# Adding the old state of a chunked recurrence in PSUM, scaling it once for each direction, and running the end of one pair of heads beside the first chain of the next

## The chip, the cores and the metric

The kernel runs on one core of a Trainium2 chip. TensorE is PE in the rows (PEld is its weight load), VectorE is DVE, ScalarE is ACT, GpSimd is POOL, and SyncE is SP, which issues the DMAs from one queue. The metric is the device time of one execution in microseconds; less is better. Before the change three runs gave 2336.16, 2346.11 and 2348.5 us, median 2346.11.

## The reference

Two residual blocks of two layers each on 512 tokens of width 1024; the second block also has 256 context tokens. The change lies in the even mixer of the second block: a linear recurrence over 768 tokens (256 of context, 512 latent) with twelve heads of 64, run forward and backward.

```python
def rwkv7_scan(r, w, k, v, kk, bb, s0, reverse):
    def step(s, inp):
        r_t, w_t, k_t, v_t, kk_t, b_t = inp
        sa = jnp.einsum('bhij,bhj->bhi', s, kk_t)
        s = s * w_t[:, :, None, :] - sa[..., None] * b_t[:, :, None, :] + v_t[..., None] * k_t[:, :, None, :]
        return s, jnp.einsum('bhij,bhj->bhi', s, r_t)
    ...
    for d in range(2):
        ...
        s_ctx, yc = rwkv7_scan(*tc[:6], zeros, d == 1)
        _, yl = rwkv7_scan(*tl[:6], s_ctx, d == 1)
def finish(o, gate_r, four, gate_f):
    mean = jnp.mean(o, axis=-1, keepdims=True)
    var = jnp.mean(jnp.square(o - mean), axis=-1, keepdims=True)
    o = ((o - mean) * lax.rsqrt(var + RWKV_GN_EPS)).reshape(b, l, RWKV_W) * lnx_g + lnx_b
    yr = o * jax.nn.silu(gate_r)
```

## The kernel before, in words

`rwkv` works on six pairs of heads (m = 0 to 5). The 128 partitions hold the two heads of a pair, 64 channels each. The 768 tokens are 12 chunks of 64, handled in three groups of four (g = 0, 1, 2), so there are 18 units of work q = 3m + g. Each unit goes through these stages, each a Python generator:

- `prep` (`inner_first`): decays and scaled keys, on ACT and DVE.
- `system` (`products`, `keys_by_token`): the products within a chunk; their triangular part goes through HBM (`lt`), POOL inverts its 16 by 16 blocks (`sN`, `sX`, `sT`), and the inverse comes back through HBM (`td`) to the tiles `T` and `DB`.
- `inverse` (`inner_rest`, `inner_second`): the 64 by 64 inverse out of these blocks, on PE (L1758), and `WT`.
- `chain`: the recurrence itself, four steps s, each with one chunk of the forward direction (d = 0) and one of the backward (d = 1). A step multiplies the old state `S` with `WT` into the PSUM tile `u` (L1822), copies `u` times -0.5 to `VU` (ACT for d = 0, DVE at L1829 for d = 1), multiplies `bkT` with `VU` into the PSUM tile `sp` (L1843), and makes the new state. Before, ACT writes the scaled old state `gs` for each direction, and four DVE instructions of 64x64 (L1851) form `sp * gc + gs`, one for each head and direction. `S` is block diagonal in the two heads. After the last step the outputs are gathered in the PSUM tile `misc` and go to `y`.

Each pair also has `pair_start` (token-major values, normalised keys) and `pair_end` (the bonus term, a normalisation over 64 channels, transposes at L1929, the gate, a store to `o_save`). `weave` emits the generators in turn. Between their steps it takes a step of `Feed`, 0.35 of one for each step of a generator: the projection matmuls of later pairs (`acc` tiles, L363 to L365, three for each slice of the depth), whose weight panels `ws` come through the SP queue. `Feed` takes its tasks strictly in the order of the list `order` and stops at one that `allow` has not yet set free; `feed.need` emits tasks until the named one is done. The framework then orders each engine's instructions by readiness. Each engine runs its own in that order.

PSUM has eight banks here: two for `acc0`, one for `acc1`, one for `misc`, two for `c`, one for `u` and one for `sp`. `misc` is shared by `prep`, `chain`, `pair_start` and `pair_end`.

Of the kernel before, what the change touches and what calls it, by code (L numbers as in the profile page):

```python
# [18 lines left out]
P = 128  # L19
# [254 lines left out]
class Program:  # L274
# [1013 lines left out]
    def rwkv(self, hl, hc):  # L1288
# [3 lines left out]
        with tc.tile_pool(name="rk", bufs=1) as rp:  # L1292
# [80 lines left out]
            order = [(0, n) for n in ("k0", "v", "r")]  # L1373
            for m in range(NH2):
                if m + 1 < NH2:
                    order.append((m, "gate"))
                    order += [(m + 1, n) for n in ("k0", "v", "r")]
            tasks = [task(*o) for o in order]
            tasks += [fourier_task(0, "four"), fourier_task(1, "four"), task(NH2 - 1, "gate"), fourier_task(0, "gate"), fourier_task(1, "gate")]
            feed = Feed(self, tasks, KT, xs)  # L1380
# [20 lines left out]
            for q in range(nq):  # L1401

                m, g = divmod(q, 3)
                gens = [self.chain(g, inner[q], pairs[m]), inverse(q + 1)]
                if g == 0:
                    if m:
                        feed.need((m - 1, "gate"))
                    run(self.pair_end(m - 1, pairs[m - 1]) if m else iter(()), system(q + 2), rate=RATE)
                    if m:
                        allow(m, "gate")  # L1410
                    start = ()
                    if m + 1 < NH2:
                        feed.need((m + 1, "v"))
                        start = self.pair_start(m + 1, pairs[m + 1])
                        feed.need((m + 1, "r"))
                    gens.append(chain(start, prep(q + 3)))
                else:
                    gens += [system(q + 2), prep(q + 3)]
                if q == nq - 1:

                    w = [rp.tile([P, 2, 2, 256], F32, tag="VU", name="dftx", bufs=2), self.E[1].rearrange("p a b -> p (a b)")]
                    for t, n in zip(w, ("k_dftx", "k_dftc")):
                        nc.sync.dma_start(out=t, in_=self.C[n])
                    feed.need(("gate", 0))
                    a = [rp.tile(sh, F32, tag=t, name=t, bufs=2) for t, sh in (("vT", [P, 6, P]), ("ks", [P, TT]))]
                    a[1] = a[1].rearrange("p (j n) -> p j n", n=P)
                    dft = lambda i, tag: self.dft(i, four["four", i], four["gate", i], a, tag, *w, tables)
                    gens.append(dft(0, "c"))
                run(*gens, rate=RATE)
                inner[q] = None  # L1430
                if g == 0:
                    allow(m + 2, "v")
                    if q == nq - 6:
                        feed.allowed.update((("four", 0), ("four", 1)))
                if g == 2:
                    allow(m + 2, "r")
                    allow(m + 3, "k0")
                    if q == nq - 4:
                        feed.allowed.update((("gate", 0), ("gate", 1)))
                if q == nq - 2:  # L1440
                    tables = [rp.tile([P, 4, T], F32, tag="m", name="m", bufs=3) for _ in range(2)]
                    for i in range(2):
                        nc.sync.dma_start(out=tables[i], in_=self.C["k_dftl"][:, :, i, :])
# [354 lines left out]
    def chain(self, g, st, pr):  # L1798
# [5 lines left out]
        Dm, VU, gc, M = self.DB, st["VU"], st["gc"], st["M"]  # L1804
        if g == 0:
            self.state = None
            pr["y"] = rp.tile([P, 6, P], F32, tag="y", name="y")
        y = pr["y"]
        u = self.psum("u", (P, 2, 2, P))
        for d, h, j, e in self.units():  # L1810
            R = half(1 - e)
# [3 lines left out]
        for s in range(4):  # L1815
# [16 lines left out]
            nxt = self.S[self.turn % len(self.S)]  # L1832
            self.turn += 1

            if S is not None:
                gs = rp.tile([P, 2, P], F32, tag="gs", name="gs")
                for d in range(2):
                    self.act(gs[:, d, :], S[:, d, :], AF.Copy, scale=gc[:, d, cs[d]:cs[d] + 1])
            yield
            sp = self.psum("sp", (P, 2, 64))  # L1840
            for d in range(2):
                for h in range(2):
                    nc.tensor.matmul(sp[half(h), d, :], st["bkT"][d][:, cs[d], half(h)], VU[:, d, cs[d], half(h)], start=True, stop=True)  # L1843
            for h in range(2):
                H = half(h)
                for d in range(2):
                    gd = gc[H, d, cs[d]:cs[d] + 1]
                    if S is None:
                        nc.vector.tensor_scalar(out=nxt[H, d, H], in0=sp[H, d], scalar1=gd, scalar2=None, op0=ALU.mult)
                    else:  # L1850
                        nc.vector.scalar_tensor_tensor(out=nxt[H, d, H], in0=sp[H, d], scalar=gd, in1=gs[H, d, H], op0=ALU.mult, op1=ALU.add)  # L1851
            self.state = nxt
            yield
        yield
        ps = self.psum("misc", (P, 4, P))

        last = None
# [33 lines left out]
    def pair_end(self, m, pr):  # L1891
# [29 lines left out]
        yield  # L1921
        tt(out=y4, in0=y4, in1=bc(s1), op=ALU.subtract)
        yield
        tt(out=y4, in0=y4, in1=bc(s2), op=ALU.mult)
        yield
        for a, b in ((0, 4), (4, 6)):
            ps = self.psum("misc", (P, 4, P))
            for j in range(a, b):
                nc.tensor.transpose(ps[:, j - a, :], y[:, j, :], self.k_ident)  # L1929
            self.act(ks[:, a * P:b * P], ps[:, :b - a, :].rearrange("p a b -> p (a b)"), AF.Identity, scale=col(cols["lgh"]), bias=col(cols["lbh"]))  # L1930
            yield
        tt(out=gate, in0=gate, in1=ks, op=ALU.mult)
# [288 lines left out]
```

## Time and profile before

| | us |
|---|---|
| median of three runs | 2346.11 |
| the profiled execution | 2352.9 |
| its span, first to last instruction | 2351.1 |
| the recurrence, about 1200 to 1912 us in the span | 712 |
| PE busy in the span | 2187.3 |
| mean granted clock of PE | 0.959 |

The granted clock is a share of 2.4 GHz: 1.00 in a stretch is 2.4 GHz throughout, 0.50 is 1.2 GHz. In rows of a timeline the first number is the start in us, the second the time to the end of the last of the xN merged instructions. An entry in brackets is how long the engine sat idle before and who released it. Matmuls are pipelined, so starts that follow each other give the pace, and the duration of one is longer.

### The profile page before, as it was taken

The numbers are of one execution on the slowest core, as the hardware profiler recorded it, in microseconds if no ns is written. First come the engines' busy times: TensorE is split into PE (matmuls) and PEld (weight loads), VectorE is DVE, ScalarE is ACT, GpSimd is POOL, SyncE is SP. The second block draws the span as 40 slices with busy tenths as digits, with TensorE's granted clock in tenths as the row PEclk, the third lists the DMA queues.
The fourth block names the chain that finished last, engine by engine and source line by source line (L and its number), as shares of the span: only waits on it lengthen the run. The fifth ranks groups of instructions, "written<-read, shape, count | busy, mean of one in ns | idle before, by whom it ended". The sixth has DMA issues, their size and how long they took to land. (4 is left out here: it accounts for less than half of the span.)

```text
span 2351.1 us, 40197 instructions
## 1 busy us (share of the span) xinstructions
PE 2187.3 (93%) x15774; PEld 1752.6 (75%) x15774; DVE 1623.3 (69%) x3014; ACT 1077.8 (46%) x2033; POOL 337.3 (14%) x722
## 2 busy tenths in 40 slices
PE   6889989999998999999898999999899999999996
PEld 4667768878775788888676677777677777888885
DVE  6799886568859787444675868787866556555544
ACT  3466353223335332333564545556554355655542
POOL 1321020000002000000004232332413100000001
PEclk9999999999999999999998979999998999999998
DMA  8433356566624656323322222212212242422211
GB/s 290 138 127 127 134 158 194 179 208 194 195 74 125 210 183 208 100 87 101 134 77 64 53 58 47 68 40 67 54 46 57 85 158 100 131 72 72 72 55 45
DMA packets 203742, 269.66 MB, mean 115 GB/s; under 512 B 125216, under 2 KB 137376, under 8 KB 203168
## 3 DMA queue, kind: packets, MB, share of 16 engines
q1 hardware_dynamic: 203552, 267.09, 37.3%
q8 instruction: 124, 2.03, 0.3%
q14 instruction: 66, 0.54, 0.1%
HBM read 250.38 MB, written 16.66 MB: 114 GB/s over the span
## 5 line engine op out<-in xcount | busy, mean ns | idle before, releaser
L363 PE MATMUL acc<-hh,wh 128*128 128x512 f32 x1416 | 574.9, 407 | 36.3 <-ACT wh L322 21.0
L365 PE MATMUL acc<-hh,wl 128*128 128x512 f32 x1416 | 571.9, 404 | 7.9 <-POOL wl L340 4.2
L364 PE MATMUL acc<-hl,wh 128*128 128x512 f32 x1416 | 572.7, 404 | 1.3 <-DVE hl L340 1.2
L322 ACT ACTIVATE wh<-ws 128x1024 fp32r<-128x1024 f32 (+4 forms) x307 | 275.8, 902 | 423.8 <-PE acc L364 313.4
L340 DVE TENSOR_TENSOR wl<-ws,wh 128x1024 fp32r<-128x1024 f32 (+3 forms) x294 | 305.3, 1041 | 202.6 <-ACT wh L322 193.7
L363 PEld LDWEIGHTS acc<-hh,wh 128*128 128x128 f32 x1416 | 271.4, 192 | 98.3 <-ACT wh L322 23.0
L365 PEld LDWEIGHTS acc<-hh,wl 128*128 128x128 f32 x1416 | 270.7, 191 | 74.6 <-DVE wl L340 8.4
L364 PEld LDWEIGHTS acc<-hl,wh 128*128 128x128 f32 x1416 | 271.6, 192 | 60.2 <-issue 5.7
L447 DVE SCALAR_TENSOR_TENSOR ws<-ws,cact 128x1024 f32<-128x1024 f32 x144 | 180.2, 1254 | 83.5 <-DMA ws<-in_ada_dram 82.3
L365 PE MATMUL acc<-gh,wl 128*128 128x512 f32 x352 | 137.9, 392 | 3.2 <-DVE wl L340 3.2
L363 PE MATMUL acc<-gh,wh 128*128 128x512 f32 x352 | 137.9, 392 | 2.2 <-ACT gh L322 2.2
L364 PE MATMUL acc<-gl,wh 128*128 128x512 f32 x352 | 138.0, 392 | 0.6 <-DVE gl L340 0.6
L322 ACT ACTIVATE a<-a 128x512 f32<-128x512 f32 x44 | 27.8, 633 | 188.4 <-DVE a L988 188.2
L1671 POOL TENSOR_TENSOR sO<-sN,sX 64x15 f32<-64x15 f32 (+2 forms) x270 | 79.7, 295 | 154.6 <-DMA sN<-lt 134.9
L1672 POOL TENSOR_TENSOR sX<-sX,sO 64x15 f32<-64x15 f32 (+2 forms) x270 | 85.1, 315 | 21.1
L2024 POOL TENSOR_TENSOR raw<-raw,k_axial 128x512 f32<-128x512 f32 x16 | 21.9, 1367 | 413.1 <-ACT raw L322 413.1
L365 PEld LDWEIGHTS acc<-gh,wl 128*128 128x128 f32 x352 | 66.5, 189 | 18.2 <-DVE wl L340 4.4
L363 PEld LDWEIGHTS acc<-gh,wh 128*128 128x128 f32 x352 | 66.4, 189 | 16.7 <-ACT gh L322 3.1
L364 PEld LDWEIGHTS acc<-gl,wh 128*128 128x128 f32 x352 | 66.5, 189 | 15.1 <-DVE gl L340 1.2
L447 DVE SCALAR_TENSOR_TENSOR ada<-ws,cact 128x1024 f32<-128x1024 f32 x48 | 58.6, 1221 | 26.5 <-DMA ws<-in_ada_dram 26.5
L1851 DVE SCALAR_TENSOR_TENSOR S<-sp,gc,gs 64x64 f32<-64x64 f32 x240 | 58.4, 280 | 20.4 <-PE sp L1843 18.7
L363 PE MATMUL acc<-hc,wh 128*128 128x256 f32 x208 | 64.3, 309 | 4.3 <-ACT wh L322 3.7
(581 smaller groups left out, 4328.4 us busy)
## 6 DMA issues: line engine op xcount, KB each, us to landing
ws<-in_ada_dram SPq DMA_DIRECT2D x144, 512.0 KB, 4.3
ws<-in_up_dram SPq DMA_DIRECT2D x88, 512.0 KB, 4.1
ws<-in_od_in_dram SPq DMA_DIRECT2D x44, 512.0 KB, 3.5
ws<-in_ev_in_dram SPq DMA_DIRECT2D x60, 256.0 KB, 2.9
ws<-in_down_dram SPq DMA_DIRECT2D x32, 384.0 KB, 3.1
ws<-in_w_in_dram SPq DMA_DIRECT2D x22, 512.0 KB, 4.5
ws<-in_down_dram SPq DMA_DIRECT2D x32, 320.0 KB, 2.9
ws<-in_ev_in_dram SPq DMA_DIRECT2D x18, 512.0 KB, 3.5
```

The source lines that it names most:

```text
L322: ins = self.nc.scalar.activation(out=out, in_=in_, func=func, **k)
L340: (engine or self.nc.vector).tensor_tensor(out=lo, in0=x, in1=hi.bitcast(F32), op=ALU.subtract)
L363: nc.tensor.matmul(ps, wh[:, s], xh, start=start, stop=False)
L364: nc.tensor.matmul(ps, wh[:, s], xl, start=False, stop=False)
L365: nc.tensor.matmul(ps, wl[:, s], xh, start=False, stop=stop)
L447: nc.vector.scalar_tensor_tensor(out=w, in0=ws, scalar=1.0, in1=c, op0=ALU.mult, op1=ALU.mult, accum_out=d[:, m:m + 1])
L1671: pt(out=ob, in0=N[:, :j, j:j + 1].to_broadcast(sh), in1=X[:, j:j + 1, j:].to_broadcast(sh), op=ALU.mult)
L1672: pt(out=X[:, :j, j:], in0=X[:, :j, j:], in1=ob, op=ALU.subtract)
L1851: nc.vector.scalar_tensor_tensor(out=nxt[H, d, H], in0=sp[H, d], scalar=gd, in1=gs[H, d, H], op0=ALU.mult, op1=ALU.add)
L2024: nc.gpsimd.tensor_tensor(out=raw, in0=raw, in1=self.k_axial[:, 0, :], op=ALU.mult)
```

## The change

Three edits. In `chain` the old state goes into `sp` by two matmuls with halves of the identity matrix (new L1835, one for each head, 256 columns for both directions), the products are added onto it in PSUM, and the sum is scaled by `gc` with one instruction of 128x128 for each direction: on DVE for d = 0 (new L1847), on ACT for d = 1. In `rwkv` the `pair_end` of the last pair no longer runs with `system` ahead of the new pair's first chain; it is put in front of `pair_start` in one generator that is woven with that chain, `inverse` and `system`. The gate task of a pair stands behind the next pair's three projections and is set free after the g = 0 run. Last, `pair_end` writes its final scaled value to `ks` instead of `y`, and `chain` takes its `y` tile later.

```diff
                 if m + 1 < NH2:
+                    order += [(m + 1, n) for n in ("k0", "v", "r")]
                     order.append((m, "gate"))
-                    order += [(m + 1, n) for n in ("k0", "v", "r")]
...
-                    run(self.pair_end(m - 1, pairs[m - 1]) if m else iter(()), system(q + 2), rate=RATE)
-                    if m:
-                        allow(m, "gate")
-                    start = ()
+                    start, end = (), self.pair_end(m - 1, pairs[m - 1]) if m else ()
...
-                    gens.append(chain(start, prep(q + 3)))
+                    gens += [system(q + 2), chain(end, start, prep(q + 3))]
...
                 if g == 0:
+                    if m:
+                        allow(m, "gate")
                     allow(m + 2, "v")
...
+            sp = self.psum("sp", (P, 2, P))
             if S is not None:
-                gs = rp.tile([P, 2, P], F32, tag="gs", name="gs")
-                for d in range(2):
-                    self.act(gs[:, d, :], S[:, d, :], AF.Copy, scale=gc[:, d, cs[d]:cs[d] + 1])
+                for h in (1, 0):
+                    nc.tensor.matmul(sp[half(h)], self.k_ident[:, half(h)], S, start=True, stop=False, skip_group_check=True)
             yield
...
+                elif d == 0:
+                    nc.vector.tensor_scalar(out=nxt[:, d, :], in0=sp[:, d, :], scalar1=gd, scalar2=None, op0=ALU.mult)
+                else:
+                    self.act(nxt[:, d, :], sp[:, d, :], AF.Copy, scale=gd)
...
-        tt(out=y4, in0=y4, in1=bc(s2), op=ALU.mult)
+        tt(out=t4, in0=y4, in1=bc(s2), op=ALU.mult)
...
-                nc.tensor.transpose(ps[:, j - a, :], y[:, j, :], self.k_ident)
+                nc.tensor.transpose(ps[:, j - a, :], ks[:, j * P:j * P + P], self.k_ident)
```

What stands in the order of PE where the second pair ends and the third begins. Before: the transposes of `pair_end` (L1929), with a run of 24 projections behind and between them; the next `u` of the chain stands 27 rows below the first transposes.

```order
L1717 MATMUL c<-VU,m 64x64 x8
L1843 MATMUL sp<-VU,bkT_11579 64x64 x2
L1929 MATMUL misc<-k_ident,y 128x128 x4
L363 MATMUL acc_12411<-hh,wh 128x512
L364 MATMUL acc_12411<-hl,wh 128x512
L365 MATMUL acc_12411<-hh,wl 128x512
L363 MATMUL acc_12411<-hh,wh 128x512
L1929 MATMUL misc<-k_ident,y 128x128 x2
L364 MATMUL acc_12411<-hl,wh 128x512
```

After, the same step of the chain (the last product into `sp` and the next `u` at L1819):

```order
L1839 MATMUL sp<-VU,bkT_11521 64x64 x2
L365 MATMUL acc_12703<-hh,wl 128x512
L365 MATMUL acc_12704<-hc_8445,wl 128x256
L363 MATMUL acc_12703<-hh,wh 128x512
L364 MATMUL acc_12703<-hl,wh 128x512
L1705 MATMUL c<-vT,k_turn 128x128 x2
L365 MATMUL acc_12703<-hh,wl 128x512
L363 MATMUL acc_12704<-hc_8445,wh 128x256
L364 MATMUL acc_12704<-hc_8446,wh 128x256
```

The transposes have moved from behind the first step of the new chain into its fourth, and 12 projections stand between the first step and the second, where before the transposes and 24 projections stood.

A step of the chain on PE in the middle of a pair. Before, then after:

```order
L1822 MATMUL u<-S_8515,WT 64x128 x2
L365 MATMUL acc_12367<-hh,wl 128x512
L363 MATMUL acc_12367<-hh,wh 128x512
L1862 MATMUL misc<-VU,m 64x64 x4
L1864 MATMUL misc<-S_8514,ar_10652 64x128
L1717 MATMUL c<-VU,m 64x64 x16
L1649 MATMUL c<-ar_11718,bk_11719 128x128
L1843 MATMUL sp<-VU,bkT_10775 64x64 x2
```

```order
L1819 MATMUL u<-S_8515,WT 64x128 x2
L1835 MATMUL sp<-S_8515,k_ident 64x256 x2
L1863 MATMUL misc<-VU,m 64x64 x4
L1865 MATMUL misc<-S_8514,ar_10710 64x128
L1716 MATMUL c<-VU,m 64x64 x16
L1648 MATMUL c<-ar_11687,bk_11688 128x128
L1839 MATMUL sp<-VU,bkT_10962 64x64 x2
```

The two identity matmuls stand directly behind the two `u` matmuls; the two projections that stood there are elsewhere.

ACT at the end of the second pair. Before, the scaled old state (`gs`) stands behind both table loads of `pair_end` and the square root between them (`hs`):

```order
L322 ACTIVATE bkT_12240<-c 128x512
L322 ACT_TABLE_LOAD
L322 ACTIVATE hs_12175<-hs_12175,eps_166 128x12
L322 ACT_TABLE_LOAD
L322 ACTIVATE hs_12175<-hs_12175 128x12
L322 ACTIVATE ks<-misc,lbh,lgh 128x512
L322 ACTIVATE gs<-S_8513,gc 128x128 x2
```

After, the new state of the backward direction stands between them:

```order
L322 ACTIVATE bkT_12389<-c 128x512
L322 ACT_TABLE_LOAD
L322 ACTIVATE hs_12332<-hs_12332,eps_166 128x12
L322 ACTIVATE S_8515<-sp,gc 128x128
L322 ACT_TABLE_LOAD
L322 ACTIVATE hs_12332<-hs_12332 128x12
L322 ACTIVATE E_8505<-EC 128x16x16
```

What has moved is a link of the chain itself: `S` is written there, and the next `u` reads it.

## Rows read from the trace of the kernel before

**Rows 1.** The page's part 1: busy time of each engine

```profile
PE 2187.3 (93%) x15774; PEld 1752.6 (75%) x15774; DVE 1623.3 (69%) x3014; ACT 1077.8 (46%) x2033; POOL 337.3 (14%) x722
```

**Rows 2.** Windows of the recurrence, 1200 to 1912 us, sum of engine times

```profile
sum 712.00, PE 658.25 PEld 508.64 DVE 517.61 ACT 369.94 POOL 208.57; mean PE 94.04 PEld 72.66 DVE 73.94 ACT 52.85 POOL 29.80
```

**Rows 3.** Windows around the five boundaries: length, engines, PEclk, DMA share, GB/s

```profile
1340.00:1370.00 30.00, 27.60 (x284) 21.79 (x283) 15.48 (x36) 8.18 (x18) 10.96 (x35) 0.58 0.24 45
1475.00:1491.00 16.00, 11.74 (x112) 9.22 (x111) 14.53 (x27) 8.51 (x15) 7.78 (x20) 0.80 0.39 86
1580.00:1600.00 20.00, 15.89 (x149) 12.79 (x141) 16.46 (x29) 10.39 (x18) 8.78 (x22) 0.83 0.44 91
1690.00:1720.00 30.00, 24.92 (x233) 20.33 (x230) 17.31 (x41) 13.97 (x29) 12.17 (x41) 0.77 0.33 69
1780.00:1810.00 30.00, 28.21 (x339) 23.05 (x335) 17.80 (x44) 9.30 (x25) 11.49 (x37) 0.66 0.27 53
sum 126.00, PE 108.36 PEld 87.19 DVE 81.58 ACT 50.36 POOL 51.18; mean PE 21.67 PEld 17.44 DVE 16.32 ACT 10.07 POOL 10.24
```

**Rows 4.** Timeline of PE, end of the second pair

```profile
1486.32 0.34 PE L1843 MATMUL sp<-VU,bkT 128*64 128x64 f32 x4 [1.08 <-DVE VU L1829]
1488.34 1.12 PE L1929 MATMUL misc<-k_ident,y 128*128 128x128 f32 x4 [1.69 <-DVE y L1924]
...
1491.90 0.40 PE L363 MATMUL acc<-hh,wh 128*128 128x512 f32 x1
1492.13 0.40 PE L364 MATMUL acc<-hl,wh 128*128 128x512 f32 x1
...
1496.55 0.44 PE L1822 MATMUL u<-S,WT 128*64 128x128 f32 x4
```

**Rows 5.** Windows of four stretches in the middle of pairs

```profile
1410.00:1475.00 65.00, 59.33 (x982) 46.09 (x982) 55.76 (x147) 35.85 (x93) 17.84 (x53) 0.97 0.21 44
...
sum 235.00, PE 220.07 PEld 172.20 DVE 202.77 ACT 138.52 POOL 57.84; mean PE 55.02 PEld 43.05 DVE 50.69 ACT 34.63 POOL 14.46
```

**Rows 6.** Groups of instructions, 1200 to 1912 us: busy us, mean ns, idle before

```profile
L1851 DVE SCALAR_TENSOR_TENSOR S<-sp,gc,gs 64x64 f32<-64x64 f32 x240 | 58.4, 280 | 20.4 <-PE sp L1843 18.7
L322 ACT ACTIVATE gs<-S,gc 128x128 f32<-128x128 f32 x120 | 42.2, 393 | 52.5 <-DVE S L1851 39.6 <-PE c L1758 10.8 <-DVE S L1849 1.5
...
L322 ACT ACTIVATE VU<-u 64x128 f32<-64x128 f32 x72 | 19.4, 269 | 38.7 <-PE u L1822 28.4 <-POOL sX L1672 5.0 <-PE u L1812 4.7
```

**Rows 7.** Timeline of DVE, one step; L895: durations min, median, max in ns

```profile
1455.11 0.98 DVE L1851 SCALAR_TENSOR_TENSOR S<-sp,gc,gs 64x64 f32<-64x64 f32 x4
...
L895 DVE COPY S<-misc x4: 277/288/292, 150.9 to 265.5; 128x128 f32<-128x128 f32 x4
```

**Rows 8.** Timeline of PE: pairs of matmuls on two halves of the array

```profile
1295.99 0.39 PE L1864 MATMUL misc<-S,ar 128*64 128x128 f32 x4
...
1335.30 0.28 PE L1864 MATMUL misc<-S,ar 128*64 128x128 f32 x1
...
1331.53 0.63 PE L1585 MATMUL c<-al,lw 64*128 64x256 f32 x1
1331.95 0.63 PE L1585 MATMUL c<-al,lw 64*128 64x256 f32 x1
```

**Rows 9.** Timeline of PE: a projection behind another form, and the next

```profile
1499.59 0.50 PE L364 MATMUL acc<-hl,wh 128*128 128x512 f32 x1
1499.93 0.40 PE L365 MATMUL acc<-hh,wl 128*128 128x512 f32 x1
```

**Rows 10.** Timeline of ACT, end of the second pair

```profile
1484.17 1.28 ACT L322 ACT_TABLE_LOAD   x1
1485.47 0.30 ACT L322 ACTIVATE hs<-hs,eps 128x12 f32<-128x12 f32 x1
```

**Rows 11.** Waits, 1200 to 1912 us (PE) and 1350 to 1912 (SP queue): us, times, longest

```profile
PE c L1758 <- DMA T<-td: 11.6, 6, 6.6
...
SPq L1934 <- DVE gate L1932: 10.8, 4, 4.4
```

More of the change, by code (lines that the diff above doesn't have):

```diff
@@ L1806, in chain @@
             self.state = None
-            pr["y"] = rp.tile([P, 6, P], F32, tag="y", name="y")
-        y = pr["y"]
         u = self.psum("u", (P, 2, 2, P))
@@ L1833, in chain @@
             self.turn += 1
+            sp = self.psum("sp", (P, 2, P))
             if S is not None:
-                gs = rp.tile([P, 2, P], F32, tag="gs", name="gs")
-                for d in range(2):
-                    self.act(gs[:, d, :], S[:, d, :], AF.Copy, scale=gc[:, d, cs[d]:cs[d] + 1])
+                for h in (1, 0):
+                    nc.tensor.matmul(sp[half(h)], self.k_ident[:, half(h)], S, start=True, stop=False, skip_group_check=True)
             yield
-            sp = self.psum("sp", (P, 2, 64))
             for d in range(2):
                 for h in range(2):
[L1843 to L1851, printed above, removed]
+                    nc.tensor.matmul(sp[half(h), d, half(h)], st["bkT"][d][:, cs[d], half(h)], VU[:, d, cs[d], half(h)], start=S is None, stop=True, skip_group_check=True)
+            for d in range(2):
+                gd = gc[:, d, cs[d]:cs[d] + 1]
+                if S is None:
+                    for h in range(2):
+                        H = half(h)
+                        nc.vector.tensor_scalar(out=nxt[H, d, H], in0=sp[H, d, H], scalar1=gd[H], scalar2=None, op0=ALU.mult)
+                elif d == 0:
+                    nc.vector.tensor_scalar(out=nxt[:, d, :], in0=sp[:, d, :], scalar1=gd, scalar2=None, op0=ALU.mult)
+                else:
+                    self.act(nxt[:, d, :], sp[:, d, :], AF.Copy, scale=gd)
             self.state = nxt
@@ L1854, in chain @@
         yield
+        if g == 0:
+            pr["y"] = rp.tile([P, 6, P], F32, tag="y", name="y")
+        y = pr["y"]
         ps = self.psum("misc", (P, 4, P))
```

## The prediction

> **What bounds the kernel now.** I read the page's busy shares first: PE works 93% of the span and DVE 69% [rows 1]. So an edit must give PE time back, or it gives nothing. Then I cut the span into windows. In the 712 us of the recurrence PE is busy 658.25 us and DVE 517.61 [rows 2], so PE idles for 53.7 us there. The granted clock is the second loss: a stretch of length L at clock c gives up L x (1 - c). Both losses pile up where one pair of heads ends and the next begins. In five windows of 126 us together PE idles 126 - 108.36 = 17.6 us, and the clock takes 30 x 0.42 + 16 x 0.20 + 20 x 0.17 + 30 x 0.23 + 30 x 0.34 = 36.3 us: 53.9 us in all [rows 3].
>
> The timeline shows how it happens at the second boundary: the first steps of the new chain wait for DVE, which at that time also does the normalisation of the old pair; PE waits 1.08 us for `VU` and 1.69 us for `y`, then it gets 24 projections almost in a row, and the next `u` starts only at 1496.55, ten microseconds after the last product of the step before [rows 4]. DVE is busy for 14.53 of the 16 us there, and much less once the projections run. In the middle of pairs it is the other way round: in four stretches of 235 us DVE is busy for 202.77 us (86%), and PE idles 14.9 us [rows 5]. So the stage alternates between stretches that DVE and the chain hold up, and stretches in which PE alone works.
>
> **The change part by part.** All durations are of one execution that took 2352.9 us, 6.8 us over the median of 2346.11; sums are made against it and carried over to the median.
>
> *Identity matmuls.* Ten of a pair's twelve steps start from an old state and make a new one, so 6 x 10 x 2 = 120 are added, 60 pairs on two halves of the array. Such halves run side by side: two pairs of 128 columns take 0.39 us, one matmul 0.28 us, so a pair costs 0.11 us and one of 256 columns 0.22 us [rows 8]. At 1.2 GHz pairs of 256 columns follow each other after 0.42 us [rows 8]. The lower end is nothing, where they run while ACT and DVE copy `u` to `VU` (0.27 us [rows 6]) and PE would idle; the upper is 60 x (0.42 + 0.22 for two changes of form, next item) = 38 us. They stand directly behind the `u` matmuls, of the same form, so I take 60 x 0.24 = +14 us.
>
> *Projections in smaller pieces.* A projection behind another form is followed after 0.34 us [rows 9]; within a run the next one follows after 0.23 us [rows 4]. So a change of form costs 0.11 us. Over the stage the new order changes between projections and the rest, or between two lines, 67 times more often (919 against 852 by my count of the order): +7 us. The bounds are 0, where PE would wait anyway, and 15 at the lower clock. On this the Trainium skill speaks against the change: TensorEngine Tiling (Array Packing), section Key Properties, says that a change of tiling mode drains the array. The 0.11 us agrees with that, but the page gives no price; with no drain the item would be 0, and by the rows it is 7.
>
> *DVE.* 240 instructions at L1851 go, 58.4 us of busy time [rows 6]; four follow each other in 0.98 us [rows 7]. In their place comes one of 128x128 out of PSUM for each step; the nearest row is a copy of that shape out of PSUM, 0.288 us [rows 7]. That frees 60 x (0.98 - 0.29) = 41 us of DVE, and makes a chain step some 0.7 us shorter. This is worth only what PE was waiting: 14.9 us in the stretches of rows 5. I take two thirds, -10 us; the ends are 0 and -15, plus their low clock, which would make it -24 (the first of them ran at 0.97 [rows 5]).
>
> *ACT.* 120 `gs` at 0.393 us go, 60 of 128x128 out of PSUM come; 64x128 out of PSUM takes 0.269 us [rows 6]. ACT, busy 52% of the stage [rows 2], gains over 25 us, which nobody waits for: 0. But its new instruction is a link of the chain, and it queues in program order. At a boundary it stands behind a table load of 1.28 us and a square root of 0.30 us [rows 10] that itself waits for DVE. That adds 1.6 to 3.2 us to one step at each of five boundaries, 8 to 16 us of chain. Behind it wait the `u` matmul of that direction, the second `VU` and the products. What hides it is the 12 projections or so that now stand between steps (12 x 0.23 = 2.8 us); I take 0, and keep 16 for the range.
>
> *The end of a pair beside the next chain.* This is the large term: the 53.9 us of rows 3. The order now spreads projections between the first four steps of the new chain, and `pair_end` trickles through DVE beside them. The gate task, moved behind the next pair's three projections, no longer blocks these, so in g = 1 and 2 there is work to draw on as well. Not all comes back: DVE still does the same normalisation there, and the first boundary begins with a wait for the inverse (`T` out of `td`, 11.6 us in six waits over the stage [rows 11]), which the change leaves. I take two thirds, -36 us; the ends are 0 and -54.
>
> *Queues.* The store of the gate to `o_save` and the two loads of `pair_start` move down the SP queue. The store already waits for its gate, 10.8 us in four boundaries, with the `td` stores of the next system queued behind it [rows 11]. If the gate comes later beside a working chain, these stores come later: 0 as long as POOL's inversion is later still; up to 10 us otherwise. POOL's own instructions keep their order but for a memset in two halves: 0.
>
> *The rest.* Writing to `ks` instead of `y`, and taking `y` later, adds no instruction; it lets the next chain's output start without the old transposes: 0.
>
> Sum: 14 + 7 - 10 - 36 = -25 us. The execution would go from 2352.9 to 2328, the median from 2346.1 to 2321 us.
>
> **The rivals.**
>
> *Full recovery.* If PE never falls idle for long at a boundary, the clock does not fall there, and all 54 us return with 15 to 24 in the stretches: 21 - 54 - 17 = -50, or 2296 us. For it: 36.3 of the 53.9 us are clock alone, and the windows with idle time are the ones with the low clock [rows 3]. Against it: even in the middle of pairs, with projections at hand, the clock is not 1.00 throughout. The Trainium skill, TensorE: Matmul & The Clock Gate, section on HAM oscillation, describes this mechanism: idle gaps in each round of a loop throttle the array each time, and a reordering that closes them wins. The rows agree that idle and low clock go together.
>
> *The wait changes its name.* PE stops waiting for `y` and waits for the inverse instead: `T` out of `td` is already its longest wait [rows 11], and the systems of g = 0 are now started beside the chain, not ahead of it. Then a third of the boundary term comes back, and -10 in the stretches stays away: 21 - 18 = +3 us, 2349 us, no change. For it: the lengths in rows 11. Against it: POOL is idle for most of the stage (208.57 of 712 us [rows 2]).
>
> *Slower: the chain hangs on ACT.* Each of the 60 new ACT instructions waits for whatever ACT has in hand, and the chain is last at every step. With a wait of 0.6 us each it adds 60 x 0.6 = 36 us; with the 21 us on PE and the 36 from the boundaries this is +21, 2367 us. It decides once the wait for ACT is longer than the 0.7 us that a step gains on DVE, and PE has no projections to put there. For it: ACT is in order and its pieces are 0.4 to 1.3 us long. Against it: `gs` waited in the same queue for the same state before, and DVE waited for it hardly at all [rows 6].
>
> **How the numbers follow.** My forecast of 2321 us gets 0.52, full recovery 0.16, the renamed wait 0.18, the chain on ACT 0.14. About 0.5% (11.7 us) is what a measurement can tell from no change, so faster is under 2334 us: 0.52 + 0.16 = 0.68; the same 0.18; slower 0.14. The forecast's own range, by the ends of its two large terms, is 2303 to 2334. The range for 8 in 10 runs from full recovery, with some 8 us below it, to a little past the renamed wait: 2288 to 2354.
>
> **What would show it.** Right: windows at the five boundaries with PE idle and clock loss of under 20 us together; DVE's busy time some 41 us lower, ACT's about 25 lower; the identity matmuls in pairs at 0.22 us; chain steps of the new pair 4 to 6 us apart with projections between them. Wrong: low clock still at every boundary; PE's longest waits for `T` or for an `S` written by ACT, in sum above 30 us; or PE's busy time up by more than 25 us at an unchanged clock.

## The result: slower, and the profile after

The changed kernel takes 2369.28 us (median of four executions) against 2347.31 for the kernel before: ratio 1.010, 95% interval 1.0065 to 1.0135. Two more comparisons gave 1.0086 (1.0059 to 1.0114) and 1.0106 (1.0058 to 1.0153). The forecast was 2321 us, 25 us faster; it is 22 us slower, outside the range of 2288 to 2354. One of the six executions of `e8` below ran at a lower clock than the others (0.944, 2401 us) and is left out of its ratio.

The page's part 1 of the changed kernel, against [rows 1]:

```profile
PE 2205.5 (93%) x16014; PEld 1754.2 (74%) x16014; DVE 1579.3 (67%) x2834; ACT 1056.9 (45%) x1973; POOL 336.2 (14%) x722
```

DVE has 44 us less work (forecast: 41) and ACT 21 less (forecast: over 25). PE has 18 more, and 240 more records, although the change adds 120 matmuls: an fp32 matmul stands in the trace as two records. I had read the counts of [rows 8] as matmuls.

The recurrence in two windows (length, then busy time and count of PE, PEld, DVE, ACT and POOL, PEclk, DMA share, GB/s), against [rows 2]:

```profile
1210.50:1570.00 359.50, 333.45 (x4300) 252.38 (x4300) 256.21 (x582) 187.28 (x423) 114.39 (x346) 0.92 0.25 56
1570.00:1929.00 359.00, 340.03 (x4383) 258.84 (x4383) 219.53 (x507) 164.59 (x372) 93.95 (x278) 0.97 0.25 61
sum 718.50, PE 673.48 PEld 511.21 DVE 475.74 ACT 351.87 POOL 208.34; mean PE 336.74 PEld 255.61 DVE 237.87 ACT 175.94 POOL 104.17
```

PE idles for 45 us of 718.5, against 53.7 of 712: the idle time did fall, and the stage became longer. The five boundaries (90 us each, from 30 us before a pair's first state is written to 60 after), against [rows 3]:

```profile
1347.70:1437.70 90.00, 84.11 (x1098) 64.89 (x1096) 62.81 (x147) 47.20 (x104) 24.75 (x74) 0.92 0.29 64
1457.70:1547.70 90.00, 83.50 (x1041) 63.70 (x1040) 59.57 (x136) 44.48 (x97) 22.39 (x70) 0.87 0.25 58
1570.30:1660.30 90.00, 80.86 (x1049) 60.93 (x1050) 59.31 (x137) 44.23 (x95) 23.47 (x70) 0.92 0.24 57
1687.80:1777.80 90.00, 84.91 (x1069) 65.59 (x1068) 57.69 (x133) 44.43 (x96) 24.09 (x70) 0.96 0.21 49
1791.30:1881.30 90.00, 86.33 (x1330) 68.55 (x1327) 49.58 (x117) 36.21 (x85) 26.44 (x74) 0.98 0.35 89
sum 450.00, PE 419.70 PEld 323.65 DVE 288.95 ACT 216.54 POOL 121.14; mean PE 83.94 PEld 64.73 DVE 57.79 ACT 43.31 POOL 24.23
```

The same five windows of the kernel before:

```profile
1351.80:1441.80 90.00, 84.33 (x1053) 64.60 (x1050) 64.72 (x156) 48.68 (x108) 24.40 (x74) 0.87 0.22 52
1458.80:1548.80 90.00, 81.90 (x1154) 63.78 (x1154) 69.08 (x169) 51.68 (x115) 26.27 (x76) 0.96 0.27 61
1564.40:1654.40 90.00, 83.34 (x1164) 64.81 (x1164) 70.74 (x173) 52.04 (x116) 26.47 (x75) 0.96 0.27 61
1665.90:1755.90 90.00, 83.21 (x1049) 66.01 (x1044) 67.14 (x165) 49.67 (x112) 24.02 (x72) 0.92 0.25 57
1785.80:1875.80 90.00, 89.41 (x1203) 69.46 (x1203) 51.03 (x133) 33.68 (x83) 22.16 (x68) 0.89 0.31 81
sum 450.00, PE 422.19 PEld 328.66 DVE 322.71 ACT 235.75 POOL 123.31; mean PE 84.44 PEld 65.73 DVE 64.54 ACT 47.15 POOL 24.66
```

PE idles for 450 - 419.70 = 30.3 us here, and for 27.8 before; the clock takes 31.5 us here and 36.0 before. So the boundaries give back next to nothing. At the first three of them the second state of a new pair now follows the first after 5 to 8 us instead of 13, as intended; at the fourth it takes 10 instead of 5. But the idle time only moved on: a step later PE waits for something else. Two of PE's waits in the stage before (us, times, longest), beside the one for `T` in [rows 11]:

```profile
PE misc L1929 <- DVE y L1924: 7.3, 4, 2.5
PE sp L1843 <- ACT VU L322: 0.4, 1, 0.4
```

and its longest ones after the change:

```profile
PE sp L1839 <- ACT VU L322: 13.7, 5, 4.6
PE c L1757 <- DMA T<-td: 12.7, 6, 5.5
PE u L1819 <- ACT S L322: 3.6, 3, 2.1
```

A long one of them, followed back at the third boundary. PE waits 4.59 us for `VU`; its timeline:

```profile
1597.18 0.48 PE L1839 MATMUL sp<-VU,bkT 128*64 128x64 f32 x4 [4.59 <-ACT VU L322]
```

ACT, which makes `VU`, waits for weights at that time:

```profile
1589.34 0.66 ACT L322 ACTIVATE WT<-c 128x256 f32<-128x256 f32 x2 [4.80 <-PE c L1791]
1594.90 0.63 ACT L322 ACTIVATE wh<-ws 128x512 fp32r<-128x512 f32 x1 [4.89 <-DMA ws<-in_ev_in_dram]
```

and these are issued late by SP's queue:

```profile
1577.05 0.33 SPq L1503 DMA_DIRECT2D r<-c_save  x1
1590.07 0.59 SPq L1675 DMA_DIRECT2D td<-sX  x1
1591.22 0.58 SPq L1675 DMA_DIRECT2D td<-sT  x1
1591.89 0.61 SPq L349 DMA_DIRECT2D ws<-in_ev_in_dram  x1
```

The queue stands still from 1577.4 to 1590.07, because the store of the small inverse waits for GpSimd, which ends `sX` at 1590.04. Behind it stands the load of a projection's weights, and behind the instruction that waits for these weights stands, in ACT's program, the copy `VU` of the new chain.

**Where the time lies.** Single executions of one kernel differ by up to 1.4% together with the clock (before: 2331.15 us at 0.972, 2363.61 at 0.960), so one trace is no verdict. The table has one trace of each kernel, and three of the two that were compared: where the stage starts (L1338), its length to the last copy of `bon`, and, over sixty equal windows from 36 us behind that start to 24 us behind that end, PE's idle time, length x (1 - granted clock), and what is left of these windows, which is PE's work at full clock. The windows are 12 us shorter together than the length beside them.

| kernel | starts at | length | idle | clock | work |
|---|---|---|---|---|---|
| before (3 traces) | 1167.0 | 720.3 | 55.5 | 51.2 | 601.5 |
| changed (3 traces) | 1170.9 | 731.4 | 46.5 | 38.7 | 634.2 |
| new order alone | 1164.2 | 708.9 | 48.4 | 42.9 | 605.6 |
| new step alone | 1170.2 | 731.5 | 51.4 | 44.1 | 624.0 |
| identity as a bare load | 1174.5 | 731.4 | 53.6 | 35.7 | 630.1 |
| the same, 128 columns | 1174.9 | 730.6 | 55.4 | 44.2 | 619.0 |

So in these traces the change did win back 9 us of idle time and 12 of clock. It paid 33 us of work on the engine that was already busy for 93% of the span.

The clock part of single traces is mostly spread. Span x granted clock, averaged over all executions, takes it out; against the kernel before, measured beside each, it is +27 us for the changed kernel (`e3` and `e16`), -7 for the new order alone, +21 for the new step alone, +29 for the identity as a bare load and +18 for the same with 128 columns. Two standard errors, about half of a 95% interval, are 3 to 4 us. Below, this is called the difference at full clock.

### The profile page after: what moved, and what is told of

Read it like the earlier page. It is cut to its first block, busy times and chain, and to the rows that moved or that the text cites. A ratio compares the mean times of both kernels' runs of the same rounds, so it can differ in the third digit from the quotient of the medians.

```text
span 2367.3 us, 40395 instructions
## 1 busy us (share of the span) xinstructions
PE 2205.5 (93%) x16014; PEld 1754.2 (74%) x16014; DVE 1579.3 (67%) x2834; ACT 1056.9 (45%) x1973; POOL 336.2 (14%) x722
## 5 line engine op out<-in xcount | busy, mean ns | idle before, releaser
L365 PE MATMUL acc<-hh,wl 128*128 128x512 f32 x1416 | 569.1, 402 | 10.5 <-DVE wl L340 5.9
L365 PEld LDWEIGHTS acc<-hh,wl 128*128 128x128 f32 x1416 | 270.3, 191 | 77.8 <-DVE wl L340 10.0
L322 ACT ACTIVATE a<-a 128x512 f32<-128x512 f32 x44 | 27.8, 633 | 207.0 <-DVE a L988 206.8
L988 DVE SCALAR_TENSOR_TENSOR a<-acc,pcol,a 128x511 f32<-128x511 f32 (+1 forms) x88 | 65.1, 745 | 0.7
```

What stands on the lines that cost most here:

```text
L322: ins = self.nc.scalar.activation(out=out, in_=in_, func=func, **k)
L365: nc.tensor.matmul(ps, wl[:, s], xh, start=False, stop=stop)
L988: nc.vector.scalar_tensor_tensor(out=a[:, j:], in0=ps[:, :T - j], scalar=cw(2 - j, f), in1=a[:, j:], op0=ALU.mult, op1=ALU.add)
```

## The experiments

**One half of the change at a time.** New order alone (`e1`, the old step put back into the changed kernel):

```diff
...
-                for h in (1, 0):
-                    nc.tensor.matmul(sp[half(h)], self.k_ident[:, half(h)], S, start=True, stop=False, skip_group_check=True)
+                gs = rp.tile([P, 2, P], F32, tag="gs", name="gs")
+                for d in range(2):
+                    self.act(gs[:, d, :], S[:, d, :], AF.Copy, scale=gc[:, d, cs[d]:cs[d] + 1])
...
```

> The changed kernel with the old recurrence step put back (two ScalarE scalings into gs, matmuls of 64 columns, four VectorE scalar_tensor_tensor): only the changed order, the end of a pair beside the next chain, and the late y and ks edits are left. Theory A (the identity matmuls cost TensorE about 26 us over 60 steps, twice what I forecast, and eat what the boundaries give back): this kernel keeps the regained idle and clock (about 29 us by the stage windows of the changed kernel, less 5 to 9 for more form changes), so it comes out near 2325, ratio 0.985 to 0.993 against before. Theory B (the boundaries give nothing; waits only change their name): ratio 0.997 to 1.003. Theory C (the woven boundaries themselves cost, and the 10.5 us that arise ahead of the recurrence belong to the new order): ratio 1.003 to 1.010.

Measured: 0.9992 (0.9966 to 1.0019). Theory B: the boundaries give nothing in time. The 7 us that it gains at full clock are lost again in the clock: the mean of its twelve executions is 0.9630, that of the kernel before beside it 0.9652, and 0.0022 of 2347 us is 5 us (a difference within noise by itself). Its trace (2340 us, near the low end of its executions, 2335 to 2356) shows 7 us less idle and 4 us more work. PE's waits in it:

```profile
PE c L1757 <- DMA T<-td: 13.5, 10, 6.0
PE acc L363 <- ACT wh L322: 4.5, 1, 4.5
PE sp L1840 <- ACT VU L322: 4.0, 6, 1.1
```

The wait for `y` at a pair's end, 7.3 us before, is gone; a wait for `wh` and more waits for `T` (10 in place of 6) have come.

New step alone (`e2`: the kernel before with only the hunks at L1829 to L1849):

> The kernel before with only the recurrence step changed (identity matmuls into sp, one scaling for each direction); order, boundaries and late edits as before. Theory A (a pair of identity matmuls of 256 fp32 columns costs TensorE 0.4 us, 60 of them 24 to 26 us; VectorE's relief of about 41 us buys back less than 10 because VectorE does not end the steps): ratio 1.006 to 1.012, about 2365. Theory as predicted (identity +14, VectorE -10): ratio 1.000 to 1.003. Theory D (the ScalarE link in the state chain and not TensorE's columns makes the cost): also 1.006 to 1.012, but TensorE's wait for S grows by more than 10 us over the stage and its busy time by under 15.

Measured: 1.0096 (1.0065 to 1.0126), the whole loss of the changed kernel, with 22.5 us more work on PE in the stage, as theory A had it; theory D had under 15. So the new step makes the kernel slower, and the new order neither adds to that in time nor takes from it. At full clock the two together (+27) cost more than their sum (+21 - 7); why is not shown.

The unchanged kernels again (`e3`, `e4`, and later `e15`, `e16`), for the spread of traces:

> The changed kernel unchanged, for a second trace of it: where does the stage of the recurrence start (the memset of zero at the start of the stage stood at 1174.1 us from the span's start, 10.5 later than in the kernel before, behind instructions in the same order)? If the 10.5 us belong to the program, it starts again 9 to 12 us later than in the second trace of the kernel before. If they are the spread of one execution, the two differ by under 4 us here, and the ratio of the two kernels stays 1.006 to 1.013 only if the recurrence itself is longer than 6 us.

> The kernel before unchanged, for a second trace of it: the stage's memset stood at 1163.6 us, its last k_sel at 1886.9, the rest of the span was 464.2. If the start is a property of the program, it is again 1162 to 1166; if it is spread, it moves by 5 us or more. Ratio 0.998 to 1.002.

> A third trace of the kernel before, for the spread of the stage's start: 1163 to 1169 if it belongs to the program, anything up to 1176 if it is the spread of single executions. Ratio 0.997 to 1.003.

> A third trace of the changed kernel: the stage starts at 1169 to 1176 if its late start belongs to the program, and may start at 1163 to 1168 if it is spread. Ratio 1.006 to 1.012.

Measured: `e3` 1.0086, `e4` 0.9979 (0.9952 to 1.0005), `e15` 1.0024 (0.9994 to 1.0055), `e16` 1.0106. The stage starts at 1164.0, 1168.5 and 1168.3 us before and at 1174.5, 1169.4 and 1168.9 after: the 10.5 us of the first two traces were mostly spread.

**What the identity matmuls cost.** The kernel before with the same matmuls into a spare part of the bank (`e6`), with half the columns (`e9`), and in one block behind the recurrence (`e10`):

```diff
+            full = self.psum("sp", (P, 384))
+            sp = full[:, :P].rearrange("p (a b) -> p a b", b=64)
+            if S is not None:
+                for h in (1, 0):
+                    nc.tensor.matmul(full[half(h), P:], self.k_ident[:, half(h)], S.rearrange("p a b -> p (a b)"), start=True, stop=True, skip_group_check=True)
...
-            sp = self.psum("sp", (P, 2, 64))
```

> The kernel before, with its ScalarE scalings, its scalar_tensor_tensor and its order untouched, and beside them the identity matmuls of the changed kernel (60 pairs, 256 columns, the same place in the order) into a spare part of the bank that nobody reads. Theory A (columns on TensorE are the whole price): as the kernel with only the new recurrence step or up to 10 slower, since here no VectorE or ScalarE work goes: ratio 1.009 to 1.014. As I forecast the identity term (0.24 us a pair, 14 us, partly in idle time): 1.000 to 1.006. Theory D (the link in the chain): 0.998 to 1.003, since nothing waits for these matmuls.

> The kernel before with the identity matmuls as a load that nobody reads (as in the run with all 256 columns, which made it 1.0120 slower), here over 128 columns for each half. Theory A (the price goes with the columns): half of it, ratio 1.004 to 1.008. Theory G (the price is that of the insertion: two more fp32 matmuls with their passes and form changes in each step, whatever their columns): 1.009 to 1.014, and then the half identity of the changed kernel could not have been faster.

> The kernel before with the same 60 pairs of identity matmuls of 256 columns in one block behind the recurrence instead of in its steps (nobody reads them). For two questions. What does a pair cost with nothing around it: theory A says 0.42 us at full clock, 25 us for 60, ratio 1.009 to 1.012; the forecast's 0.24 says 14 us, 1.005 to 1.007. And does the stage of the recurrence start late (1169 to 1175 in the six kernels with identity matmuls in the steps, 1164 to 1169 in four without), although nothing ahead of it differs: if that hangs on the length of TensorE's program alone, it starts at 1169 to 1175 here too.

Measured: `e6` 1.0120 (1.0088 to 1.0152), `e9` 1.0049 (1.0022 to 1.0076), `e10` 1.0155 (1.0098 to 1.0211). Theory A holds for the first two: the price goes with the columns, and it does not fall into PE's idle time (53.6 us in the table, 55.5 before). `e10` lies above theory A's range, though its interval reaches into it. In `e10` the block of 60 pairs stands in PE's timeline as one row:

```profile
1890.06 26.12 PE L1447 MATMUL sp<-S,k_ident 128*64 128x256 f32 x240
```

26.12 / 60 = 0.435 us a pair at a granted clock of 1.00, where I had reckoned 0.22. The Trainium skill, FP8 and Floating Point Precision, section TensorE Precision Notes, says that a true FP32 product takes four passes through the array. An estimate from it, 256 columns x 4 at 2.4 GHz, is 0.427 us, and the row agrees with that.

**Half the identity in the changed kernel** (`e5`: the diagonal blocks alone, and so four scalings of 64x64 for a step), and the same four scalings with the full identity (`e13`, whose edit this is; in `e5` the identity matmuls read `S[:, :, half(h)]` as well):

```diff
-                elif d == 0:
-                    nc.vector.tensor_scalar(out=nxt[:, d, :], in0=sp[:, d, :], scalar1=gd, scalar2=None, op0=ALU.mult)
-                else:
-                    self.act(nxt[:, d, :], sp[:, d, :], AF.Copy, scale=gd)
+                else:
+                    for h in range(2):
+                        H = half(h)
+                        if d == 0:
+                            nc.vector.tensor_scalar(out=nxt[H, d, H], in0=sp[H, d, H], scalar1=gd[H], scalar2=None, op0=ALU.mult)
+                        else:
+                            self.act(nxt[H, d, H], sp[H, d, H], AF.Copy, scale=gd[H])
```

> The changed kernel with the identity matmuls over the diagonal blocks only (64 columns of each direction, 128 in place of 256 for each half) and, as that leaves sp with blocks of 64, four scalings of 64x64 for each step (two on VectorE, two on ScalarE). Theory A (the price is TensorE's columns): half of about 24 us comes back, 2355 to 2360, ratio 1.003 to 1.006 against the kernel before, and TensorE's full-clock work in the stage falls from 634 by 10 to 13. Theory D (the ScalarE link in the state chain makes the loss; it is still there, with two ScalarE instructions for each step where there was one): no better than the changed kernel, ratio 1.008 to 1.013.

> The changed kernel with its identity matmuls over all 256 columns, but the scaling of each direction split into two of 64x64 (two on VectorE, two on ScalarE), as in the kernel with half the identity. If the four small scalings (VectorE 0.56 in place of 0.35 us, ScalarE 0.62 in place of 0.36 for each of 60 steps) are what ate the half of the columns there: 10 to 25 us slower than the changed kernel, ratio 1.013 to 1.020. If they cost nothing: 1.007 to 1.012, and the price of the halved identity's kernel lies elsewhere.

Measured: `e5` 1.0148 (1.0113 to 1.0183), `e13` 1.0192 (1.0157 to 1.0226). `e5` alone spoke against the price of columns; `e13` explains it. Four small scalings cost 14 to 20 us more than two (`e13` against the changed kernel measured beside it, `e16`; 12 at full clock). Half the columns then save about 10 us, within the noise of the two ratios; at full clock 8 (+31 against +39, to within 6). PE's work in the stage fell by only 4 us in `e5`, from 634.2 to 630.4, where theory A had 10 to 13. The timelines show one way in which the small scalings cost time. One of the longer steps of the changed kernel:

```profile
1654.00 0.35 DVE L1847 TENSOR_SCALAR S<-sp,gc 128x128 f32<-128x128 f32 x1 [0.29 <-PE sp L1839]
...
1654.87 0.35 ACT L322 ACTIVATE S<-sp,gc 128x128 f32<-128x128 f32 x1
...
1655.19 0.51 PE L1819 MATMUL u<-S,WT 128*64 128x128 f32 x4
...
1655.46 0.67 PE L1835 MATMUL sp<-S,k_ident 128*64 128x256 f32 x4
```

and one of the longer of `e13`:

```profile
1658.27 0.57 DVE L1850 TENSOR_SCALAR S<-sp,gc 64x64 f32<-64x64 f32 x2
...
1658.99 0.30 ACT L322 ACTIVATE S<-sp,gc 64x64 f32<-64x64 f32 x1
...
1660.08 0.31 ACT L322 ACTIVATE S<-sp,gc 64x64 f32<-64x64 f32 x1
...
1660.40 0.43 PE L1819 MATMUL u<-S,WT 128*64 128x128 f32 x2
```

The two directions are not scaled side by side. ACT's scaling starts after the end of DVE's in each of the 60 steps, and in 21 of them over 0.3 us after it, behind whatever ACT has in hand. From the start of the first to the end of the second it takes 1.22 us in this step, 2.12 in that of `e13`. These two are not typical: over all 60 steps the median is 0.75 us in the changed kernel (mean 1.26, longest 8.56) and 1.31 in `e13` (mean 1.92); four `scalar_tensor_tensor` took 0.98 (mean 1.09). The groups of the changed kernel (busy us, mean ns, idle before and what ended it) show ACT waiting for DVE, against [rows 6]:

```profile
L1835 PE MATMUL sp<-S,k_ident 128*64 128x256 f32 x240 | 43.8, 399 | 0.0
...
L322 ACT ACTIVATE S<-sp,gc 128x128 f32<-128x128 f32 x60 | 21.8, 363 | 39.1 <-DVE S L1847 38.8
L1847 DVE TENSOR_SCALAR S<-sp,gc 128x128 f32<-128x128 f32 x60 | 20.9, 348 | 20.8 <-PE sp L1839 20.0
```

Whether it is the bank of `sp` or the tile `S`, which both share, that orders the two was not tried.

**Is it the link through ACT?** Both scalings on DVE (`e7`):

```diff
-                elif d == 0:
-                    nc.vector.tensor_scalar(out=nxt[:, d, :], in0=sp[:, d, :], scalar1=gd, scalar2=None, op0=ALU.mult)
                 else:
-                    self.act(nxt[:, d, :], sp[:, d, :], AF.Copy, scale=gd)
+                    nc.vector.tensor_scalar(out=nxt[:, d, :], in0=sp[:, d, :], scalar1=gd, scalar2=None, op0=ALU.mult)
```

> The changed kernel with the second direction's scaling moved from ScalarE to VectorE, so that the state chain has no ScalarE instruction left between sp and S. Theory A: within 5 us of the changed kernel, ratio 1.007 to 1.012. Theory D: the waits for VU and S on ScalarE (17 us in the stage of the changed kernel, with their clock) go, 2345 to 2357, ratio 0.999 to 1.005.

Measured: 1.0157 (1.0120 to 1.0195). Theory D is out: with ACT off the link the kernel is no faster, rather slower, though both scalings now take 0.6 us together. PE's wait for the `VU` of ACT did not go either: 19.7 us in its trace, against 13.7. At full clock it is +31 us, against +27 for the changed kernel, within noise of each other; whether it is slower at all stays open.

**What is a boundary worth?** The kernel before, where the transposes at a pair's end do not wait (`e8`; it leaves the normalised rows out of the gate):

```diff
-                nc.tensor.transpose(ps[:, j - a, :], y[:, j, :], self.k_ident)
+                nc.tensor.transpose(ps[:, j - a, :], vT[:, j, :], self.k_ident)
```

> The kernel before, with the six transposes at the end of a pair reading vT, which is ready early, in place of y: TensorE doesn't wait for the normalised rows there (so y's normalisation doesn't reach the gate's product). It is the most that taking this wait off TensorE's path can give without any weaving. My forecast's boundary term (two thirds of 54 us of idle and lost clock): ratio 0.984 to 0.992. Theory E (only the idle that stands directly at these transposes is to be had, four waits of 1.4 to 2.6 us, about 8 us with as much clock again at most; the chain behind the boundary makes the others): ratio 0.994 to 0.999. Theory F (the waits move to the next chain's sp and T matmuls): 0.998 to 1.002.

Measured: 1.010 (1.0052 to 1.0148), slower, outside all three theories and nearest to F. PE's waits in its trace (of its fastest execution, 2351 us):

```profile
PE c L1758 <- DMA T<-td: 17.1, 10, 6.5
PE acc L363 <- DVE v L1322: 14.1, 3, 4.7
PE sp L1843 <- DVE VU L1829: 8.0, 10, 1.3
```

The 7.3 us of waiting for `y` are gone, and three waits of 4.7 us have come: PE reaches the projections sooner and finds their bank not yet emptied, since DVE is in the middle of the same normalisation. That DVE's work at the boundary is the cause, and that the order only decides which of PE's instructions waits for it, fits this trace; no run takes that work away. Of the loss of some 25 us, 8 remain at full clock (to within 6); the rest is a lower clock, 0.959 on average against 0.966.

**SP's queue.** The stores of the small inverse issued by GpSimd, which makes it, in the changed kernel (`e11`) and in that with the new order alone (`e12`):

```diff
-            nc.sync.dma_start(out=blocks(td[k]), in_=x)
+            nc.gpsimd.dma_start(out=blocks(td[k]), in_=x)
```

> The changed kernel with the two stores of the small inverse (td<-sX, td<-sT) issued from GpSimd, which makes sX, in place of SyncE's queue, where they wait for it for up to 17 us with the projections' weight loads behind them. Theory H (these loads come late, ScalarE waits for ws and holds VU, and this is where the boundaries' gain goes): ScalarE's wait for ws (11 to 14 us in the stage) falls below 4, TensorE's for VU (13.7) below 7, and the time falls by 8 to 20 us: ratio 1.000 to 1.006 against the kernel before. Theory F (another wait takes its place): within 5 us of the changed kernel, 1.007 to 1.012.

> The kernel with the new order and the old recurrence step (0.9992 against before), with the two stores of the small inverse issued from GpSimd. If SyncE's queue holds back what the new order could give, 0.988 to 0.995; if not, 0.997 to 1.002.

Measured: 1.0113 (1.0062 to 1.0163) and 1.0053 (1.0015 to 1.0091): no gain in the one, a loss in the other, outside both ranges. In the trace of `e11` ACT waits 5.3 us for weights instead of 11.4, and PE

```profile
PE c L1757 <- DMA T<-td: 20.1, 11, 6.7
PE sp L1839 <- ACT VU L322: 8.7, 4, 3.4
```

The wait for `VU` fell by 5 us and that for `T` rose by 7. Theory F once more. But the edit did not free SP's queue. Its waits in `e11`:

```profile
SPq L1733 <- DMA td<-sX: 128.3, 14, 16.7
SPq L1733 <- DMA td<-sT: 51.3, 12, 20.0
```

The loads of `T` and `DB` (L1733) stand in the same queue and now wait there for the stores that have left it, with the weight loads behind them: 179.6 us, where in the changed kernel the stores waited 173.9 us for GpSimd (both from 1210 to 1910 us). What a queue without this stall would give was not tried.

**Ahead of the stage.** The table shows kernels with identity matmuls starting the stage late, behind instructions that are the same. `e14` is `e10` with 16 columns for each matmul:

> The kernel before with 120 identity matmuls of 16 columns (240 records, as many as the changed kernel has more) in one block behind the recurrence, their outputs unread: 240 records of about 0.06 us, 10 to 15 us of TensorE by themselves. If the length of TensorE's program makes the stage of the recurrence start late, it starts at 1170 to 1176 and the ratio is 1.006 to 1.010; if not, at 1163 to 1169 and 1.003 to 1.007.

Measured: 1.0108 (1.0074 to 1.0142), with a block of 8.43 us; GpSimd's timeline at the start of the stage:

```profile
1176.40 0.57 POOL L1338 MEMSET E<- 128x512 f32 x1
```

Over all traces the stage starts at 1166.5 on average in the six of kernels without the 240 records (1164.0 to 1169.8), and at 1172.4 in the twelve of kernels with them (1168.0 to 1176.4), wherever in the program they stand. About 4 of these 6 us are idle time of PE ahead of the stage, 82.0 us on average against 77.8, and one wait there separates the two groups: that for `gh` out of ACT is 2.2 to 5.4 us in the six and 6.2 to 9.0 in the twelve. So some 6 us of the loss go with the 240 records. What carries them is open.

This also accounts for most of what the four bare loads cost beside their own work. At full clock they cost +18 us (`e9`), +29 (`e6`), +32 (`e10`) and +13 (`e14`). Their own work is about 13, 26, 26 and 7 us (the block of `e14` ran at 0.83), and the 3 to 6 us left are of the size of the later start. The rest of `e14`'s loss is clock: 0.9605 on average, against 0.9649 beside it.

## Why the prediction was wrong

The forecast was +14 +7 -10 -36. The runs gave about +28 for the identity; -6 for the relief of DVE and ACT (1.0096 against 1.0120, not distinguishable from 0; -8 at full clock, to within 4); and -2 for the new order as a whole, where +7 - 36 = -29 was forecast (-7 at full clock).

- *Identity matmuls, +14: half of what they cost.* I divided one row of [rows 8] by the wrong count: four records are two matmuls, one pair, and not two pairs. The cost is 0.435 us a pair, 26 us, and `e6` shows that no idle time hides it. The upper end of 38 us held by luck, for the same miscount is in it: the two rows 0.42 us apart are one matmul, so that a pair at 1.2 GHz takes twice that.
- *Projections in smaller pieces, +7: about right.* The new order alone adds some 4 us of work in the table; the change has 33, where the new step alone has 22.5.
- *DVE, -10: the freed time was right (44 us, forecast 41) and the gain of 6 to 8 us not far off, but not by the way that I gave.* "Makes a chain step some 0.7 us shorter" failed: the second scaling waits for the first, and the pair takes 0.75 us at the median and 1.26 on average, against 0.98 and 1.09. In `e7` the pair takes 0.6 us, and the kernel is no faster.
- *The end of a pair beside the next chain, -36: this step failed most.* I took the idle time and the low clock at the boundaries to be what the order cost, two thirds of which a new order would give back. Of the idle time `e1` won 7 us in its trace; of the clock, which is 36.3 of the 53.9 us, nothing came back in the mean of its executions (0.9630, before 0.9652). `e1`, `e8` and `e11` each took a wait away or shortened it and found another longer. The rival in which the wait changes its name described this; it named one new wait, and there were three (`T`, `VU`, `wh`). That they are the price of DVE's and ACT's work, the inverse and the weight loads in any order is likely, but only two orders were tried. The reading that the windows with idle time are the ones with the low clock does not hold in [rows 3] either: the two lowest clocks, 0.58 and 0.66, stand where PE idles least (2.4 and 1.8 of 30 us). What lowers the clock there stays open.
- *Queues, 0 to 10:* the stall on SP's queue was real: ACT waits 11 to 15 us for weights in the changed kernel's traces, 2.5 before. In the case that I followed it stood at a store of the inverse. The queue's wait for the gate, which I had named, rose as well, from 10.8 to some 27 us. `e11` moved the stall to another place in the queue, and gave nothing.
- *The rival with the chain on ACT came within 2 us of the measured time, by luck:* it had 36 us of waiting for ACT, and over the 60 steps ACT's scaling does start 33 us in sum after the end of DVE's, 14 of them in two steps. But `e7`, which takes ACT out of this link, gains nothing. A matching number says little while another sum gives it too.
- *Not in the forecast:* the later start of the stage.
- *The forecast's own range, 2303 to 2334, was too narrow for its terms:* with the boundaries alone at their end of 0, which their item allows, the sum gives 2357.

## What to carry to other kernels

Before you price an instruction by a row, check the row's count against the code: here one fp32 matmul is two records, and that alone was 12 us. Work that was moved onto the engine which is busy for 93% of the span was paid in full here, however idle the engines were that it relieved. Where executions differ in their clock, compare span x granted clock beside the times: it told 7 us from nothing here. Idle time at a seam belongs to a chain of several engines; before you count on it, take the one wait away in a throwaway kernel, look whether it is really gone, and see whether the time comes back or another wait does.

## What the hardware showed that I had not expected

- A pair of fp32 matmuls on two halves of the array takes 0.435 us for 256 columns (`e10`) at a granted clock of 1.00, and still 8.43 / 60 = 0.14 for 16 (`e14`) at 0.83.
- 240 more records of TensorE behind the recurrence, 8.43 us of work, made the kernel before 1.0108 (1.0074 to 1.0142) slower, some 25 us and so more than their own time; the order of the instructions ahead of them had not changed. At full clock 13 us of it remain, to within 5.
- Taking a wait of 7 us off TensorE did not raise the clock: the five executions of `e8` that its ratio counts ran at 0.951 to 0.970, those of the kernel before beside it at 0.960 to 0.971.
